# Expert stage of a hybrid layer: 128-column stationary tiles, a new order for the first two experts, filler products

## The chip, the core and the metric

The kernel runs on one core of one Trainium2 chip. The metric is the device time of one execution in microseconds. Its engines are named as in the profile: PE multiplies matrices, ACT and DVE work on tiles element by element, POOL and SP mostly issue transfers here, and 16 DMA engines move the data.

## What is computed

One transformer layer over 512 tokens of 1024 values in fp32: a gated linear attention, a sparse attention and an attention over a memory, mixed by gates, and then a mixture of 16 experts. The change lies in the mixture. Each token chooses one of four groups and two of its four experts, and the two experts' results are added with weights that come from the routing:

```
def _hier_moe(h, w_r1, b_r1, w_r2, b_r2, w_gate, w_up, w_down):
    ...
    g_sel = jnp.argmax(g_logits, axis=-1)
    ...
    top_p, top_i = lax.top_k(e_prob, EXPERT_TOPK)          # 2 of 4 in the group
    top_p = top_p / jnp.sum(top_p, axis=-1, keepdims=True)
    expert_id = g_sel[:, None] * EXPERTS_PER_GROUP + top_i
    combine = jnp.sum(jax.nn.one_hot(expert_id, N_EXPERTS, dtype=jnp.float32)
                      * (g_w * top_p)[..., None], axis=1)
    hid = jax.nn.silu(jnp.einsum('nd,edf->nef', hf, w_gate)) * jnp.einsum('nd,edf->nef', hf, w_up)
    hid = hid * combine[..., None].astype(hid.dtype)
    out = jnp.einsum('nef,efd->nd', hid, w_down)
```

The experts' hidden width is 256, so one expert has 1024 x 256 gate and up weights and 256 x 1024 down weights, 3 MB.

## The kernel before

**Split products.** Most products are made from fp32 values split into two parts of a shorter type, h and l (`split_into`, L92 to L99: ACT casts h, DVE subtracts to get l). `mm3` (L101 to L104) adds three PE products of such parts: h by h (L102), h by l (L103) and l by h (L104). In the trace's rows for the experts the stationary operand is named second: g<-wh,xgh is the PSUM tile g from the moving weights wh and the stationary tokens xgh, and "128*96" in such a row is 128 rows by 96 stationary columns. The gate stage of the attention part uses the same three products (L155, L160, L161) with 128 columns.

**Experts.** A routing stretch on PE, DVE and ACT (`route`, `place`, `weigh`, `spread`, `rows`, `weights`, L1107 to L1249) places each expert's tokens into C = 96 slots and writes their indices to `idx0` (L1243). For each expert `gather` (L1278) has POOL issue an indirect transfer that fetches the 96 token rows into one of two buffers. `tokens_t` (L1285) transposes them on PE in eight blocks (L1291) and splits the result, four blocks at a time, into xgh and xgl; the last block stays fp32 as xgr. `up` (L1311) runs one of four steps kc over the 1024 inputs: steps 0 to 2 are six split products each, step 3 is the fp32 products of xgr (L1323, two per expert, four records in the trace) and three split products. `hidden` (L1328) applies silu, the product and the routing weights `cwt0`, `hidden_t` (L1335) transposes the hidden values (L1338) and splits them into hh and hl, and `down` (L1344) makes six split products for each half c of the output. `scatter` (L1353) copies the result (ACT, L1355) and has POOL issue an indirect transfer that adds it into the output (L1356). So an expert has 21 + 12 = 33 split products. Expert 0's tokens come by products with one-hot matrices (L1172) and not by a gather, and its first PRE = 2 steps' weights are split ahead of time (eh, el).

**Order.** The scheduler of the language takes instructions in the order in which the loop over the experts emits them. A string of letters steers the loop (L1368 to L1393): a digit is a step of `up` for expert e, h its `hidden`, t `tokens_t` for expert e+1, and H, a, b are `hidden_t` and both halves of `down` for expert e-1; the last expert has a string of its own, LAST.

```
ORDER = "0H12at3bh"
...
            elif op == "t" and e + 1 < ne:
                xt[e + 1] = tokens_t(got[e + 1])
```

The routing weights (`weights`, L1245) come from four products (L1229) whose moving operand `aux` DVE makes (L1226), and are reduced by DVE to `cwt` (L1249). A count of tokens per expert (L1397) at the end decides whether a branch for more than 96 tokens runs; it does not run on these inputs. `WARM` = 8 products into an unused tile (`idle`, L1256) stand ahead of the last part of the routing.

**Weights.** `load_expert` (L858) issues an expert's 12 tiles of 256 KB on SP's queue, in order, into slots of one pool (tag "s", NS = 66, 2 KB a partition each); `fetch` runs NF = 4 experts ahead. The last HB = 2 tiles of expert 3 wait for `idx0` ("gathers first"), and all behind them in SP's queue with them. A tile is cast (L94) and split (L95) into one of WH = 3 pairs wh, wl. The tiles of tokens (tag "x", 4 buffers) and hidden values (tag "u", NU = 6) have as many columns as an expert has slots, 96.

## Time and profile before

| | us |
|---|---|
| median of 3 runs | 957.44 |
| lowest and highest run | 955.07, 958.75 |
| the profiled execution, its own time | 958.75 |
| its span in the trace | 957.0 |
| PE busy | 923.3 |
| DVE busy | 646.4 |
| ACT busy | 467.0 |
| POOL busy | 136.0 |

The profile is of one execution. A row of the timeline gives start and duration of an instruction in microseconds from the start of the span, its engine, its line in the kernel, what it writes from what it reads, its shape, and in brackets how long its engine stood idle ahead of it and what ended that. Matmuls are pipelined on PE, so the distance between the starts of two of them is the time that one takes, and the duration in the row is longer. A row of windows gives, for a stretch, the busy time and number of instructions of each engine, the granted clock of PE (1.00 is the full one), the share of the DMA engines' time that was in use, and what they moved.

### The profile page before, as it was taken

How to read it: one execution, taken by the hardware profiler on the slowest of the kernel's cores; microseconds unless marked ns; L12 is line 12 of the kernel's file. 1: busy time of each engine (PE TensorE's matmuls, PEld its weight loads, DVE VectorE, ACT ScalarE, POOL GpSimd, SP SyncE). 2: the span in 40 equal slices, each digit the busy share in tenths (PEclk: the TensorE clock that was granted, in tenths of full speed). 3: DMA queues.
4: the chain of work that ended last, by engine and by line, in shares of the span. 5: the costliest groups of instructions: out<-in, count | busy, mean ns of one | idle time of the engine just before them, and what ended most of it. 6: DMA issues, size and time to landing. Idle time of an engine off the chain costs nothing.

```text
span 957.0 us, 13025 instructions
## 1 busy us (share of the span) xinstructions
PE 923.3 (96%) x4408; PEld 747.7 (78%) x4408; DVE 646.4 (68%) x1602; ACT 467.0 (49%) x935; POOL 136.0 (14%) x120
## 2 busy tenths in 40 slices
PE   8898999999999999999999999999999988999994
PEld 5678888787888888887888888878888876777773
DVE  6785689869988595458545552573463667898983
ACT  5664546435323354455513423443324336888883
POOL 4000122000500050000000000000003122434332
PEclk9998999999999999999999999999999979999998
DMA  7744431312333223221332233215847439999992
GB/s 224 243 114 130 124 89 45 89 44 67 93 107 92 87 67 86 69 73 38 88 89 91 86 88 88 88 45 175 286 145 234 151 134 291 326 317 314 303 321 50
DMA packets 75063, 133.79 MB, mean 140 GB/s; under 512 B 10640, under 2 KB 13278, under 8 KB 74992
## 3 DMA queue, kind: packets, MB, share of 16 engines
q1 hardware_dynamic: 66656, 119.56, 39.9%
q0 software_dynamic: 7152, 11.25, 4.9%
q10 hardware_dynamic: 1184, 2.11, 0.6%
q8 instruction: 36, 0.59, 0.3%
q14 instruction: 35, 0.29, 0.1%
HBM read 125.59 MB, written 10.49 MB: 142 GB/s over the span
## 4 chain that ended last, share of the span: by engine, by line
PE 81%; DVE 9%; ACT 3%; DMA 3%; issue 2%; POOL 0%; SPq 0%; POOLq 0%; ACTq 0%; DVEq 0%
PE g L160 18%; PE g L155 18%; PE g L161 18%; PE g L104 4%; PE g L103 4%; PE g L102 4%; DVE wl L95 2%; PE g L1323 1%; PE tp L1291 1%; ACT wh L94 1%; PE g L1172 1%; DMA wr<-in_w_mem_kv_dram 1%; DMA hx<-in_x_dram 1%; PE tp L103 1%; PE lg L1095 1%
## 5 line engine op out<-in xcount | busy, mean ns | idle before, releaser
L94 ACT CAST wh<-wr 128x1024 fp32r<-128x1024 f32 (+2 forms) x125 | 127.6, 1024 | 277.5 <-PE g L160 160.6
L95 DVE TENSOR_TENSOR wl<-wr,wh 128x1024 fp32r<-128x1024 f32 (+2 forms) x125 | 152.3, 1220 | 154.1 <-ACT wh L94 152.6
L155 PE MATMUL g<-hh,wh 128*128 128x512 f32 (+1 forms) x424 | 167.7, 395 | 3.1 <-DVE mvl L98 1.9
L160 PE MATMUL g<-hl,wh 128*128 128x512 f32 (+1 forms) x424 | 166.1, 392 | 0.0
L161 PE MATMUL g<-hh,wl 128*128 128x512 f32 (+1 forms) x424 | 165.6, 391 | 0.0
L95 DVE TENSOR_TENSOR wl<-mw,wh 128x512 fp32r<-128x512 f32 (+1 forms) x188 | 112.6, 641 | 9.2 <-ACT wh L94 8.3
L94 ACT CAST wh<-mw 128x512 fp32r<-128x512 f32 (+1 forms) x188 | 100.9, 588 | 11.5 <-PE g L104 10.8
L155 PEld LDWEIGHTS g<-hh,wh 128*128 128x128 f32 x424 | 80.7, 190 | 18.4 <-DVE mvl L98 2.2
L161 PEld LDWEIGHTS g<-hh,wl 128*128 128x128 f32 x424 | 80.6, 190 | 15.1
L160 PEld LDWEIGHTS g<-hl,wh 128*128 128x128 f32 x424 | 80.7, 190 | 14.1
L160 PE MATMUL g<-wl,hh 128*128 128x512 f32 x160 | 63.1, 394 | 0.0
L155 PE MATMUL g<-wh,hh 128*128 128x512 f32 x160 | 63.1, 394 | 0.0
L161 PE MATMUL g<-wh,hl 128*128 128x512 f32 x160 | 62.9, 393 | 0.0
L1356 POOL DMA_INDIRECT out_dram<-y,idx x32 | 45.5, 1421 | 91.3 <-ACT y L1355 87.4
L102 PE MATMUL g<-wh,xgh 128*96 128x512 f32 x108 | 46.7, 433 | 0.0
L476 POOL PARTITION_ALL_REDUCE dqsq<-dqsq x8 | 26.3, 3364 | 127.0 <-ACT dqsq L468 127.0
L104 PE MATMUL g<-wh,xgl 128*96 128x512 f32 x108 | 42.8, 397 | 0.0
L103 PE MATMUL g<-wl,xgh 128*96 128x512 f32 x108 | 42.6, 395 | 0.0
L987 POOL MEMSET tmp<- 128x128 f32 x1 | 0.2, 206 | 290.8 <-PE tp L822 290.8
L160 PEld LDWEIGHTS g<-wl,hh 128*128 128x128 f32 x160 | 30.2, 189 | 6.2 <-issue 0.5
L155 PEld LDWEIGHTS g<-wh,hh 128*128 128x128 f32 x160 | 30.1, 188 | 6.3 <-issue 0.5
L645 ACT ACTIVATE dp<-dp,nm,rs_y 128x128 f32<-128x128 f32 (+3 forms) x32 | 20.9, 654 | 28.5 <-DVE nm L644 28.5
(424 smaller groups left out, 1991.9 us busy)
## 6 DMA issues: line engine op xcount, KB each, us to landing
wr<-in_w_in_dram SPq DMA_DIRECT2D x72, 512.0 KB, 3.5
mw<-in_w_gate_dram SPq DMA_DIRECT2D x64, 256.0 KB, 7.6
mw<-in_w_up_dram SPq DMA_DIRECT2D x64, 256.0 KB, 7.8
mw<-in_w_down_dram SPq DMA_DIRECT2D x64, 256.0 KB, 7.5
wr<-in_w_mem_kv_dram SPq DMA_DIRECT2D x16, 512.0 KB, 6.3
wr<-in_w_o_mem_dram SPq DMA_DIRECT2D x8, 512.0 KB, 3.6
wr<-in_w_o_dsa_dram SPq DMA_DIRECT2D x8, 512.0 KB, 3.6
wr<-in_w_o_gla_dram SPq DMA_DIRECT2D x8, 512.0 KB, 4.2
```

The costliest lines, as they stand in the source:

```text
L94: hi = A.copy(h, src)
L95: lo = V.tensor_sub(l, src, h.bitcast(F32))
L102: PE.matmul(ps, sh, mh, start=first, stop=False)
L103: PE.matmul(ps, sh, ml, start=False, stop=False)
L104: PE.matmul(ps, sl, mh, start=False, stop=last)
L155: i = PE.matmul(ps, sh, mh, start=first, stop=False)
L160: PE.matmul(ps, sh, ml, start=False, stop=False)
L161: i = PE.matmul(ps, sl, mh, start=False, stop=last)
L476: G.partition_all_reduce(flat, flat, P, bass_isa.ReduceOp.add)
L645: A.activation(p, p, AF.Exp, bias=nm[:, t:t + 1], scale=rs, accum_out=sm[:, t:t + 1])
L1095: PE.matmul(pl, hT[:, k, :], wr[:, kb, :], start=k == 0, stop=k == 3)
L1356: nc.gpsimd.indirect_dma_start(out=out[c], in_=y, in_offset=None, compute_op=OP.add, out_offset=bass.IndirectOffsetOnAxis(ap=idx0[:, e:e + ...
```

## The change

The stationary tiles of tokens and hidden values become buffers that are allocated once, with 128 columns, of which the last 32 are set to zero once (seven memsets on DVE); every product of `up` and `down` now has 128 stationary columns, and its PSUM tile 128 rows, of which the first 96 are read. `tokens_t` becomes a generator of two parts: t makes the eight transposes and splits the first four blocks, u splits the rest. There are strings of their own for expert 0 (FIRST) and expert 1 (SECOND), so that all of expert 0's steps come ahead of expert 1's transposes. Those transposes, and WARM = 4 filler products ahead of them, are held behind the last product of expert 0's step 3 and the last product of the routing weights (`after_all`). The 8 idle products ahead of the routing remain. The weights' pool grows from 66 to 72 slots; for that the space for the descriptors of indirect transfers is cut from 16384 bytes a partition, the default, to 4096.

```diff
@@ -31,14 +31,14 @@
 TAKEN = -(2.0 ** 127)
 NEG = -1e30
 
-NS, NU, WR, WH = 66, 6, 4, 3
+NS, NU, WR, WH = 72, 6, 4, 3
 AHEAD, NF = 2, 4
 E0, HB = -1, 2
-ORDER = "0H12at3bh"
+FIRST, SECOND, ORDER = "0123htu", "Ha012bt3uh", "0H12at3ubh"
 LAST = "0H12a3hbGcd"
 N1, N2 = 8, 8
 PRE = 2
-WARM = 8
+WARM = 4
 L0, L2, LW, LA = 2, 2, 2, 2
 SB, MS, MB, D1, D2, DB, GS = 12, 3, 6, 12, 10, 16, 9
 WA, WB = 12, 17
@@ -101,7 +101,7 @@
     def mm3(ps, sh, sl, mh, ml, first, last):
         PE.matmul(ps, sh, mh, start=first, stop=False)
         PE.matmul(ps, sh, ml, start=False, stop=False)
-        PE.matmul(ps, sl, mh, start=False, stop=last)
+        return PE.matmul(ps, sl, mh, start=False, stop=last)
 
     def wconv(raw, w):
         h = wp.tile([P, 2, w], F32R, tag="wh", name="wh", bufs=WH)
@@ -1226,8 +1226,9 @@
         V.tensor_mul(aux, sel[:, tt, :, :].rearrange("p t c e -> p (t c) e").to_broadcast([P, 4, 16, n]),
                      vals[:, tt, :, o:o + n].rearrange("p t c v -> p (t c) v")[:, :, None, :].to_broadcast([P, 4, 16, n]))
         for k in range(4):
-            PE.matmul(ps, ohs[t0 // 2][:, k, :], aux[:, k, :, :].rearrange("p e c -> p (e c)"),
+            end = PE.matmul(ps, ohs[t0 // 2][:, k, :], aux[:, k, :, :].rearrange("p e c -> p (e c)"),
                       start=t0 == 0 and k == 0, stop=last and t0 == 2 and k == 3)
+        return end
 
     def rows(idx):
         pi = ap_.tile([C, 16 * 3], F32, tag="lg", name="lg")
@@ -1245,14 +1246,15 @@
     def weights(ohs, cwt):
         pw = ap_.tile([C, 16 * 6], F32, tag="lg", name="lg")
         for t0 in (0, 2):
-            spread(pw, ohs, 3, 6, t0, True)
+            end = spread(pw, ohs, 3, 6, t0, True)
         V.tensor_reduce(cwt, pw.rearrange("p (e q c) -> p e q c", q=2, c=3), axis=AX.X, op=OP.add)
+        return end
 
     out_gemm()
     run(fill[0])
 
     idle = gp.tile([P, 512], F32, tag="g", name="g")
-    for _ in range(WARM):
+    for _ in range(8):
         PE.matmul(idle, mgH[0][:, 0:P], mgH[0], start=True, stop=True)
     rest = place(2)
     run(islice(rest, N2))
@@ -1282,31 +1284,38 @@
                                      bounds_check=T - 1, oob_is_err=False)
         return xb[e % 2]
 
+
+    xs = [[sp.tile([P, 4, P], F32R, tag="x", name="xg" + n, bufs=4) for n in "hl"] for _ in range(2)]
+    xraw = sp.tile([P, P], F32, tag="xr", name="xgr", bufs=1)
+    hhl = [half([P, 2, P], F32R, "h" + n) for n in "hl"]
+    for t in xs[0] + xs[1] + hhl:
+        V.memset(t[:, :, C:P].bitcast(F32), 0.0)
+    V.memset(xraw[:, C:P], 0.0)
+
     def tokens_t(xg, placed=None, m=C):
+
         xH, xL = [], []
+        tps = placed
+        if placed is None:
+            tps = [ap_.tile([P, 4, m], F32, tag="tp", name="tp") for _ in range(2)]
+            for kb in range(KB):
+                PE.transpose(tps[kb // 4][:, kb % 4, :], xg[:, :, kb], ident[0:m, 0:m])
         for c in range(2):
-            if placed is None:
-                tp = ap_.tile([P, 4, m], F32, tag="tp", name="tp")
-                for k in range(4):
-                    PE.transpose(tp[:, k, :], xg[:, :, 4 * c + k], ident[0:m, 0:m])
-            else:
-                tp = placed[c]
-            h = sp.tile([P, 4, m], F32R, tag="x", name="xgh", bufs=4)
-            l = sp.tile([P, 4, m], F32R, tag="x", name="xgl", bufs=4)
-            raw = sp.tile([P, m], F32, tag="xr", name="xgr", bufs=2) if c else None
+            tp = tps[c]
+            h, l = xs[c]
             n = 4 - c
             if placed is None:
-                split_into(h[:, 0:n, :], l[:, 0:n, :], tp[:, 0:n, :])
+                split_into(h[:, 0:n, 0:m], l[:, 0:n, 0:m], tp[:, 0:n, :])
             else:
                 for k in (0, 2):
                     q = min(k + 2, n)
-                    split_into(h[:, k:q, :], l[:, k:q, :], tp[:, k:q, :])
-            if c:
-                A.copy(raw, tp[:, n, :])
+                    split_into(h[:, k:q, 0:m], l[:, k:q, 0:m], tp[:, k:q, :])
             xH += [h[:, k, :] for k in range(4)]
             xL += [l[:, k, :] for k in range(4)]
-        xL[KB - 1] = raw
-        return xH, xL
+            if c:
+                A.copy(xraw[:, 0:m], tp[:, n, :])
+                xL[KB - 1] = xraw
+            yield xH, xL
 
     def up(ps, xH, xL, ws, kc, done=None):
         nk = 1 if kc == 3 else 2
@@ -1323,28 +1332,28 @@
                 PE.matmul(ps[:, i * 256:(i + 1) * 256], xL[KB - 1], ws[4 * i + kc][:, 1, :], start=False, stop=False)
         for k in range(nk):
             kb = 2 * kc + k
-            mm3(ps, xH[kb], xL[kb], *parts[k], kb == 0, kc == 3)
+            end = mm3(ps, xH[kb], xL[kb], *parts[k], kb == 0, kc == 3)
+        return end
 
     def hidden(ps, cwt, m=C):
         hid = half([m, P, 2], F32, "hid")
         hf = hid.rearrange("p i k -> p (i k)")
-        A.activation(hf, ps[:, 0:256], AF.Silu, scale=cwt[:, 1:2])
-        V.scalar_tensor_tensor(hf, ps[:, 256:512], cwt[:, 0:1], hf, op0=OP.mult, op1=OP.mult)
+        A.activation(hf, ps[0:m, 0:256], AF.Silu, scale=cwt[:, 1:2])
+        V.scalar_tensor_tensor(hf, ps[0:m, 256:512], cwt[:, 0:1], hf, op0=OP.mult, op1=OP.mult)
         return hid
 
     def hidden_t(hid, m=C):
         tp = ap_.tile([P, 2, m], F32, tag="tp", name="tp")
         for k in range(2):
             PE.transpose(tp[:, k, :], hid[:, :, k], ident[0:m, 0:m])
-        hh = half([P, 2, m], F32R, "hh")
-        hl = half([P, 2, m], F32R, "hl")
-        split_into(hh, hl, tp)
+        hh, hl = hhl
+        split_into(hh[:, :, 0:m], hl[:, :, 0:m], tp)
         return hh, hl
 
-    def down(hh, hl, ws, c, m=C):
+    def down(hh, hl, ws, c):
         wh = wp.tile([P, 2, 512], F32R, tag="wh", name="wh", bufs=WH)
         wl = wp.tile([P, 2, 512], F32R, tag="wl", name="wl", bufs=WH)
-        ps = gp.tile([m, 512], F32, tag="g", name="g")
+        ps = gp.tile([P, 512], F32, tag="g", name="g")
         for k in range(2):
             split_into(wh[:, k, :], wl[:, k, :], ws[8 + 2 * c + k])
             mm3(ps, hh[:, k, :], hl[:, k, :], wh[:, k, :], wl[:, k, :], k == 0, k == 1)
@@ -1352,7 +1361,7 @@
 
     def scatter(e, c, ps):
         y = yb[e % 2][:, c, :]
-        A.copy(y, ps)
+        A.copy(y, ps[0:C, :])
         nc.gpsimd.indirect_dma_start(out=out[c], in_=y, in_offset=None, compute_op=OP.add,
                                      out_offset=bass.IndirectOffsetOnAxis(ap=idx0[:, e:e + 1], axis=0),
                                      bounds_check=T - 1, oob_is_err=False)
@@ -1363,27 +1372,35 @@
     with tc.issue_after(late[LW].ins):
         weigh(2)
     with tc.issue_after(late[LA].ins):
-        weights(ohs0, cwt0)
-    xt[0] = tokens_t(None, x0)
+        weighed = weights(ohs0, cwt0)
+    xt[0] = list(tokens_t(None, x0))[1]
     for e in range(ne):
         if e + NF < ne:
             fetch(e + NF, after=found if e == E0 else None)
         if e + 2 < ne:
             got[e + 2] = gather(e + 2)
-        for op in ORDER if e < ne - 1 else LAST:
+        for op in {0: FIRST, 1: SECOND, ne - 1: LAST}.get(e, ORDER):
             if op in "0123":
                 if op == "0":
-                    ps = gp.tile([C, 512], F32, tag="g", name="g")
+                    ps = gp.tile([P, 512], F32, tag="g", name="g")
                 kc = int(op)
                 if e == 0 and kc >= PRE:
                     with tc.issue_after(late[2].ins):
-                        up(ps, *xt[e], wts[e], kc)
+                        end = up(ps, *xt[e], wts[e], kc)
                 else:
                     up(ps, *xt[e], wts[e], kc, pre if e == 0 else None)
             elif op == "h":
                 hid[e] = hidden(ps, cwt0[:, e, :])
             elif op == "t" and e + 1 < ne:
-                xt[e + 1] = tokens_t(got[e + 1])
+                with after_all([end, weighed] if e == 0 else []):
+                    if e == 0:
+                        for _ in range(WARM):
+                            PE.matmul(idle, xs[0][0][:, 0, :], xs[0][0].rearrange("p k c -> p (k c)"),
+                                      start=True, stop=True)
+                    halves = tokens_t(got[e + 1])
+                    xt[e + 1] = next(halves)
+            elif op == "u" and e + 1 < ne:
+                next(halves)
             elif op in "HabGcd" and e + (op in "Gcd") > 0:
                 o = e if op in "Gcd" else e - 1
                 if op in "HG":
@@ -1422,7 +1439,7 @@
                 V.tensor_copy(cx, cw[:, t, one, :].rearrange("p o q -> p (o q)"))
                 xg = wp.tile([P, P, KB], F32, tag="wr", name="xg", bufs=WR)
                 nc.sync.dma_start(xg.rearrange("p i k -> p (i k)"), h2d[rs, :])
-                xH, xL = tokens_t(xg, m=P)
+                xH, xL = list(tokens_t(xg, m=P))[1]
                 ps = gp.tile([P, 512], F32, tag="g", name="g")
                 for kc in range(4):
                     up(ps, xH, xL, ws, kc)
@@ -1430,7 +1447,7 @@
                 for c in range(2):
                     o = slot([P, 512], F32, "o")
                     nc.sync.dma_start(o, out[c][rs, :])
-                    V.tensor_add(o, o, down(hh, hl, ws, c, P))
+                    V.tensor_add(o, o, down(hh, hl, ws, c))
                     nc.sync.dma_start(out[c][rs, :], o)
 
 
@@ -1445,7 +1462,8 @@
     import concourse.bacc as bacc
     from concourse.bass_utils import run_bass_kernel_spmd
 
-    nc = bacc.Bacc("TRN2", target_bir_lowering=False, num_devices=1)
+    nc = bacc.Bacc("TRN2", target_bir_lowering=False, num_devices=1,
+                   dynamic_dma_scratch_size=4096)
     arrays, args = {}, {}
     for name in _INS:
         v = np.ascontiguousarray(np.asarray(inputs[name])[0])
```

Three places show how the instructions move. On PE, behind step kc 2 of expert 0, before the change (lg<-aux are the products of the routing weights, tp<-ident,xg the transposes of expert 1's tokens, and the numbers are the stationary columns by the moving ones; transposes are listed the other way round):

```order
L104 MATMUL g<-wh,xgl 96x512
L1291 MATMUL tp<-ident,xg 128x96 x8
L1323 MATMUL g<-mw,xgr 96x256 x2
L102 MATMUL g<-wh,xgh 96x512
L103 MATMUL g<-wl,xgh 96x512
L104 MATMUL g<-wh,xgl 96x512
L102 MATMUL g<-wh,xgh 96x512
L1229 LDWEIGHTS oh
L1229 MATMUL lg<-aux_7255,oh 96x96
```

On PE at the same place after the change (L1414 is the count, L1398 the fillers, L1302 the transposes of expert 1's tokens and L1348 those of expert 0's hidden values):

```order
L1414 LDWEIGHTS ones_b
L1414 MATMUL lg<-sel_6454,ones_b 128x16
...
L1332 MATMUL g<-mw,xgr 128x256 x2
L102 MATMUL g<-wh,xgh 128x512
L103 MATMUL g<-wl,xgh 128x512
L104 MATMUL g<-wh,xgl 128x512
L1229 LDWEIGHTS oh
L1229 MATMUL lg<-aux_7269,oh 96x96
...
L1398 MATMUL g<-xgh 128x512 x4
L1302 MATMUL tp<-ident,xg 128x96 x8
L1348 MATMUL tp<-ident,hid 128x96 x2
L102 MATMUL g<-wh,hh 128x512
```

The count comes from the end of the kernel to this place, the transposes of expert 1 go behind expert 0's step kc 3, the products of the routing weights and the fillers, and the down products of expert 0 come right behind, ahead of all of expert 1's steps.

On DVE in the same stretch, before the change (aux_7255 is the operand of the routing weights' last products, pr and vals are parts of the routing):

```order
L1208 TENSOR_TENSOR pr<-pr,vals 128x4
L95 TENSOR_TENSOR wl<-mw,wh 128x2x256
L1209 CAST vals<-pr 128x4
L95 TENSOR_TENSOR xgl<-tp,xgh 128x384
L1226 TENSOR_TENSOR aux_7255<-sel,vals 128x384
L95 TENSOR_TENSOR wl<-mw,wh 128x2x256
L1249 TENSOR_REDUCE cwt_7136<-lg 96x32
L95 TENSOR_TENSOR xgl<-tp,xgh 128x288
```

On DVE after it (cmaxi is the highest count, hl the lower part of the hidden values):

```order
L1208 TENSOR_TENSOR pr<-pr,vals 128x4
L95 TENSOR_TENSOR wl<-mw,wh 128x2x256
L1209 CAST vals<-pr 128x4
L1418 CAST cmaxi<-cmax 128x1
L1226 TENSOR_TENSOR aux_7269<-sel,vals 128x384
L95 TENSOR_TENSOR wl<-mw,wh 128x2x256
L1250 TENSOR_REDUCE cwt_7136<-lg 96x32
L95 TENSOR_TENSOR wl<-mw,wh 128x2x256
L1342 SCALAR_TENSOR_TENSOR hid<-g,cwt_7136,hid 96x256
L95 TENSOR_TENSOR xgl<-tp,xgh 128x4x96
L95 TENSOR_TENSOR xgl<-tp,xgh 128x3x96
L95 TENSOR_TENSOR hl<-tp,hh 128x2x96
```

The operand of the routing weights no longer stands behind the split of expert 1's tokens, and both halves of that split stand directly ahead of the split of expert 0's hidden values.

## Rows read from the trace of the kernel before

**Rows 1.** The page, busy time of each engine, its share and number of instructions:

```profile
PE 923.3 (96%) x4408; PEld 747.7 (78%) x4408; DVE 646.4 (68%) x1602; ACT 467.0 (49%) x935; POOL 136.0 (14%) x120
```

**Rows 2.** Windows of the expert stage: PE, PEld, DVE, ACT, POOL, clock, DMA, GB/s:

```profile
820.00:840.00 20.00, 20.00 (x99) 14.79 (x98) 18.00 (x34) 17.53 (x40) 7.89 (x6) 1.00 1.01 323
936.00:938.00 2.00, 2.00 (x10) 1.43 (x9) 1.75 (x4) 1.51 (x3) 0.00 (x0) 1.00 0.26 56
```

**Rows 3.** Timeline of PE: transposes of experts 2 and 15, first product of expert 2:

```profile
803.32 1.02 PE L1291 MATMUL tp<-ident,xg 96*128 96x96 f32 x8
804.18 1.03 PE L1323 MATMUL g<-mw,xgr 128*96 128x256 f32 x4
804.86 0.58 PE L102 MATMUL g<-wh,xgh 128*96 128x512 f32 x1
...
807.13 0.39 PE L102 MATMUL g<-wh,xgh 128*96 128x512 f32 x1
...
927.86 1.02 PE L1291 MATMUL tp<-ident,xg 96*128 96x96 f32 x8
```

**Rows 4.** Timeline of PE, head of the expert stage:

```profile
787.22 0.40 PE L102 MATMUL g<-eh,xgh 128*96 128x512 f32 x1
...
790.46 0.39 PE L104 MATMUL g<-wh,xgl 128*96 128x512 f32 x1
793.25 1.30 PE L1291 MATMUL tp<-ident,xg 96*128 96x96 f32 x8 [2.40 <-DMA xg<-h2d,idx]
...
797.34 0.39 PE L102 MATMUL g<-wh,xgh 128*96 128x512 f32 x1
```

**Rows 5.** Windows of the head, columns as in rows 2:

```profile
790.00:794.00 4.00, 1.59 (x10) 1.07 (x9) 1.79 (x7) 0.62 (x1) 0.00 (x0) 0.99 0.89 220
794.00:796.00 2.00, 2.00 (x9) 1.47 (x7) 1.46 (x3) 1.00 (x2) 0.96 (x1) 0.50 0.98 296
```

**Rows 6.** Timeline of PE, gate stage, first and last of 37 products in a row:

```profile
742.59 0.39 PE L155 MATMUL g<-wh,mgh 128*128 128x512 f32 x1
...
750.78 0.39 PE L155 MATMUL g<-wh,mgh 128*128 128x512 f32 x1
```

**Rows 7.** Groups of loads, 720 to 957: count, busy us, mean ns, idle before:

```profile
L103 PEld LDWEIGHTS g<-wl,xgh 128*96 128x96 f32 x108 | 17.6, 163 | 6.4
...
L155 PEld LDWEIGHTS g<-wh,mgh 128*128 128x128 f32 x54 | 10.2, 188 | 1.7
```

**Rows 8.** Timeline of DVE in the head:

```profile
794.54 0.56 DVE L95 TENSOR_TENSOR xgl<-tp,xgh 128x384 fp32r<-128x384 f32 x1 [2.22 <-ACT xgh L94]
795.01 0.55 DVE L1226 TENSOR_TENSOR aux<-sel,vals 128x384 bf16<-128x384 bf16 x1
```

**Rows 9.** Timeline of POOL, issue of the gather for expert 1:

```profile
786.24 1.33 POOL L1280 DMA_INDIRECT xg<-h2d,idx  x1 [15.91 <-DVE rr L1208]
```

**Rows 10.** Waits of SP's queue, 785 to 800: total us, times, longest:

```profile
SPq L866 <- PE tp L1291: 2.4, 1, 2.4
```

**Rows 11.** Timeline of SP, issue of a weight tile of expert 15:

```profile
923.02 0.33 SPq L866 DMA_DIRECT2D mw<-in_w_up_dram  x1
```

**Rows 12.** The page, transfers: count, KB each, median us from issue to landing:

```profile
mw<-in_w_up_dram SPq DMA_DIRECT2D x64, 256.0 KB, 7.8
```

**Rows 13.** Timelines of ACT and PE, expert 15's step kc 1:

```profile
931.54 0.63 ACT L94 CAST wh<-mw 128x512 fp32r<-128x512 f32 x1
...
933.21 0.45 PE L102 MATMUL g<-wh,xgh 128*96 128x512 f32 x1
```

**Rows 14.** Timeline of DVE in the routing stretch:

```profile
781.47 0.22 DVE L1153 TENSOR_TENSOR ppc<-sel,lg 128x64 f32<-128x64 bf16 x1 [2.65 <-PE lg L1151]
```

**Rows 15.** Timeline of PE, last head of the sparse attention:

```profile
429.78 0.55 PE L662 MATMUL tp<-ident,dp 128*128 128x128 f32 x3 [0.25 <-DVE dol L95]
```

**Rows 16.** Waits, 800 to 940, columns as in rows 10:

```profile
DVE wl L95 <- DMA mw<-in_w_gate_dram: 0.6, 2, 0.3
```

**Rows 17.** Scatters by their line, L1356: time to landing in the whole span:

```profile
DMA to landing us min/median/max: 4.1/7.0/8.0
```

## Prediction

> **What bounds the kernel now.** I read the page first: PE is busy for 923.3 of 957.0 us [rows 1], so time can only come from PE's own work or from the few places where it stands still. The change touches two stretches. In the expert stage PE is full, 20.00 us of 20, while the DMA engines are full as well, share 1.01 at 323 GB/s [rows 2]. One expert takes (927.86 - 803.32) / 13 = 9.58 us on PE, from one expert's transposes to the next one's [rows 3]. The other stretch is the head of that stage: the last split product of expert 0's step kc 2 starts at 790.46, and the next thing in PE's row, expert 1's transposes, at 793.25, after 2.40 us of idle time put down to the gather of expert 1's tokens [rows 4]. [...]
>
> What that head costs: from 793.25 to 797.34 PE ran eight transposes, the fp32 products and three split products in 4.09 us [rows 4]. At the full clock the transposes and fp32 products of expert 2 took 804.86 - 803.32 = 1.54 us [rows 3], and three split products take 0.69, so 2.23 us. The slow clock costs 1.86 us and the idle time 2.40, together 4.3 us. No more than that can be had in the head.
>
> **The change part by part.**
>
> *128 columns.* Products with 96 stationary columns follow each other by (790.46 - 787.22) / 14 = 231.4 ns [rows 4]; products of the gate stage with 128 columns by (750.78 - 742.59) / 36 = 227.5 ns [rows 6]. There are 33 split products per expert, 528 in all; 528 x 3.9 ns = 2.1 us less. Zero is the other end, if the 4 ns belong to the gate stage and not to the columns; I take 2.0, since operation, type and moving size are the same. The load of the stationary tile gets longer, from 163 to 188 ns in the mean [rows 7]. If the 25 ns came on top, they would cost 528 x 25 = 13 us; but both loads are shorter than the spacing, and with 188-ns loads the gate stage still kept 227.5 ns, so they lie beside the products. [...]
>
> *Head.* Expert 0's last products, the count of tokens per expert and the products that gather the routing weights go ahead of expert 1's transposes, and four filler products stand behind them. I walk PE's row from 790.69, where 790.46's slot ends. Four count products cost at most 0.43 us, since expert 2's eight transposes start 0.86 us ahead of its fp32 products [rows 3]. Then kc 3 of expert 0: 1.54 - 0.86 = 0.68 for the fp32 products and 0.69 for three split ones, to 792.5. The weight products need an operand from DVE. Before, that ran at 795.01, behind a split that had waited 2.22 us for the transposed tokens and began at 794.54 [rows 8]; so DVE was free at 792.3. In the new order one more split and three short operations are ahead of it, and it is ready at 793.1 to 793.7: PE waits some 0.9 us. Four weight products take at most 0.43 again, four fillers 0.91, and the transposes begin at 794.7, when the gather has landed, if it is issued at 786.24 [rows 9] and lands by 793.25 as before; they end at 795.6. ACT and DVE then split two halves of the tokens and the hidden values in turn, so the first down product waits about 0.7 us, to 796.3 (an estimate from the 0.56 us of one half's split [rows 8]). Thirty products at 0.2275 are 6.8 us, transposes and fp32 products 1.54, three products 0.69: expert 2's first product comes at 805.4 instead of 807.13 [rows 3]. That is 1.7 us, of which 0.14 (36 products by 3.9 ns) is in the 2.0 above already. The stretch also had small waits that the walk leaves out, so I take 1.3 us. The high end is 1.6; the low end is -0.3, if the two waits bring the half clock back as the 2.40 us did (1.86 us). What is late next is the split of the hidden values.
>
> *72 slots for weights.* In the head SP waited once, for 2.4 us, for PE's transposes to free a slot [rows 10], and the DMA share was 0.89 in 790 to 794 [rows 5]. Six more slots of 256 KB let SP issue past that. To be had is the missing share, 0.11 of 4 us, 0.4 us, since from 794 on it is 0.98 and over. I take 0.4 (the other end is 0): earlier weights, not yet an earlier end.
>
> *The cap.* PE's gain is 2.0 + 1.3 = 3.3 us. But the weights come at the rate of the DMA engines, which are full nearly to 936 (1.01 in 820 to 840, 0.26 in 936 to 938 [rows 2]); a PE that is 3.3 us ahead would meet them. At expert 15 the kc 1 tile of in_w_up was issued at 923.02 [rows 11], and with the median of 7.8 us to landing [rows 12] it came at about 930.8. ACT cast it at 931.54, and PE started on that step at 933.21 [rows 13]. A cast at the landing would let PE come 0.7 us earlier, and some 0.4 of the 1.67 between cast and step can go (the cast is 0.63, and DVE's half of the split about as long): 1.1 us in all, and 0.4 from the slots. So 1.5 of the 3.3 us reach the end; the ends are 0 and 3.7 (2.1 + 1.6).
>
> *Costed at nothing.* Seven memsets of padding columns run on DVE, most of them in the routing stretch, where it stood idle for 2.65 us ahead of 781.47 [rows 14]; if all fell on the way to the gather's indices they would cost 7 x 0.19 = 1.3 us (an estimate: a third of the 384-column split's 0.56). The second half of the token split moves behind kc 3, which reads the same buffers, so it could not run sooner. In the last head of the sparse attention, near 430 us, the scheduler spreads filler work differently; PE waits there for 0.25 us at a time [rows 15], and two such waits, 0.5 us either way, are my allowance. The count leaves the tail, where PE waited for the hidden values anyway.
>
> **The sum.** The profiled run took 958.75 us (span 957.0). Less 1.5 it is 957.2. The median of the runs, 957.44, stands 1.3 below the profiled run; less 1.5 it is 955.9 us.
>
> **Rivals.**
>
> *The weights do not bind.* Their last tiles come sooner than the median or the casts close up, and all 3.3 us stay: 954.1. For it: in 800 to 940 DVE waited for gate tiles only twice, 0.6 us in all [rows 16]. Against it: the full DMA share.
>
> *It doesn't do what it says.* The idle time goes over from the gather to the weight operand and the hidden split, at the half clock, and the 4 ns are not the columns': 957.4 + 0.3 = 957.7, and up to 959.5 with memsets (1.3) and the reorder (0.5). For it: the walk has PE waiting 1.6 us in place of 2.40. Against it: the spacings in rows 4 and 6 differ steadily over 14 and 36 products.
>
> *Everything lands.* The whole 4.3 us of the head less 0.9 for the fillers, 2.1 from the columns and no cap: 5.5 us, 951.9. It needs the weight operand and the hidden split on time; the walk has them 0.9 and 0.7 late.
>
> *Slower: GpSimd's transfers queue for descriptor space.* The change cuts the space for descriptors of indirect transfers from 16384 to 4096 bytes a partition. The place is POOL's queue, with two scatters and a gather per expert. If one must land before the next is written, each costs its way to landing, 7.0 us in the median for a scatter [rows 17]; three are 21 us, 11.4 over the 9.58 of an expert, and 14 experts add 160 us: some 1115. With two in flight three take 10.5 us, 0.9 over, and add 13 us: 970. It decides from 3.2 us per transfer. Against it: POOL is busy for 7.89 of 20 us [rows 2], so it has room, but nothing shows how full the space is. [...]
>
> **How the numbers follow.** Chances: the capped forecast 0.50, no cap 0.20, no effect 0.14, everything lands 0.10, slower through the descriptors or a load that is not hidden 0.06. A measurement of this kernel can tell about 0.5%, 4.8 us, from no change: under 952.65 counts as faster, over 962.2 as slower. Faster is most of the case where everything lands and the low edge of the uncapped one, 0.12; slower is 0.07 with the edge of no effect; the same 0.81. The range goes from 951.5 (everything lands, with 0.4 from the reorder near 430 us) to 959.5 (no effect, with memsets and reorder); it leaves out the descriptor case and edges of the others.
>
> **What the profile of the changed kernel would show.** PE's idle time ahead of expert 1's transposes should be near 1 us and owed to DVE, no window after 790 should show 0.50, and expert 2's first product should start between 805.3 and 806. Products should follow each other by 227 to 228 ns, an expert take 9.45 us, and then, in the last three experts, ACT or DVE should wait for gate and up weights: that is the cap. If there are no such waits and PE ends 3 us earlier, the cap is wrong. If 0.50 stays in 794 to 800, the head is wrong; if the spacing stays at 231, the columns give nothing; if POOL waits for DMA between gathers, the descriptors are short, and the forecast is wrong by most.

## The result and the profile after

The changed kernel took 948.63 us in the median of 7 runs (947.74 to 953.18), the kernel before 957.44 (955.07 to 961.52) in 7 runs beside them: ratio 0.9905, 95% interval 0.9887 to 0.9923, so 8.8 us faster. The forecast was 955.9, "the same", with a range down to 951.5. The time lies below the range.

The profiled run of the changed kernel was the longest of its seven (953.18 us, span 951.24). Its first products of the memory attention began at 10.86 us where they began at 8.51 before, and from there on it ran late. So the same kernel was run once more ("after_r" below: 949.5 us in the median, and 949.5 in its profiled run, span 947.57), and the rows "of after" come from that profile, unless the text says otherwise.

The page of after, busy times and granted clock in 40 slices:

```profile
PE 917.9 (97%) x4412; PEld 756.3 (80%) x4412; DVE 645.4 (68%) x1609; ACT 467.8 (49%) x935; POOL 136.5 (14%) x120
...
PEclk9999999999999999999999999999999999999998
```

The same line of the page of before, which the prediction did not use:

```profile
PEclk9998999999999999999999999999999979999998
```

PE's busy time fell by 5.4 us against [rows 1]; its weight loads grew by 8.6 us and lie beside the products. The 7 in slice 33 (some 765 to 789 us: the routing of the last token tiles, ahead of the expert stage) is gone. The prediction began its account of PE at 786 and passed over this slice. (The 8 in slice 4 comes and goes from run to run: the first profile of the changed kernel has it too.)

Both profiles, cut at the same instructions on PE (us; each cell is a difference of two starts in the timeline):

| stretch | before | after | difference |
|---|---|---|---|
| start to the last gate product ahead of the last routing products | 765.37 | 763.75 | -1.6 |
| routing: from there to expert 0's first product | 21.10 | 15.20 | -5.9 |
| head: from there to expert 3's transposes | 26.43 | 26.13 | -0.3 |
| expert 3's transposes to the last product | 131.15 | 133.76 | +2.6 |
| last product to the last scatter's issue | 3.89 | 2.52 | -1.4 |
| last scatter's issue to the end of the span | 9.02 | 6.21 | -2.8 |

The first line says nothing of the change: the changed kernel's own two profiles stand at 768.25 and 763.75 there. The gain lies in the routing and behind the last scatter, two places for which the prediction had no gain at all.

*The routing.* Windows of before, columns as in [rows 2] (PE, PEld, DVE, ACT, POOL busy, clock, DMA share, GB/s), and the same windows of after:

```profile
764.00:768.00 4.00, 1.90 (x11) 1.28 (x10) 3.79 (x16) 1.23 (x6) 3.21 (x5) 1.00 0.71 229
768.00:772.00 4.00, 3.65 (x26) 3.44 (x27) 2.95 (x26) 3.83 (x13) 1.84 (x2) 0.75 0.82 295
772.00:776.00 4.00, 4.00 (x21) 4.00 (x20) 0.99 (x10) 0.00 (x0) 0.00 (x0) 0.50 0.46 180
```

```profile
764.00:768.00 4.00, 3.33 (x30) 2.97 (x30) 3.21 (x23) 4.00 (x14) 1.84 (x2) 1.00 0.45 177
768.00:772.00 4.00, 4.00 (x33) 3.82 (x33) 2.72 (x27) 0.31 (x1) 0.00 (x0) 1.00 0.09 35
772.00:776.00 4.00, 2.66 (x24) 2.14 (x23) 3.47 (x22) 0.00 (x0) 0.00 (x0) 1.00 0.00 0
```

Before, PE stood still for more than half of 764 to 768, and then worked at a granted clock of 0.75 and 0.50. After, it did neither. The timelines of before tell why it stood still: POOL, DVE, ACT and PE, one fence each.

```profile
761.76 2.53 POOL L1077 TENSOR_TENSOR xg<-xr,gffn 128x512 f32<-128x512 f32 x2 [19.12 <-PE g L160]
...
765.37 1.28 POOL L1077 TENSOR_TENSOR xg<-xr,gffn 128x512 f32<-128x512 f32 x1
```

```profile
762.01 1.05 DVE L1182 TENSOR_SCALAR neg<-gt 128x2 f32<-128x2 f32 x1
...
763.17 1.14 DVE L1122 TENSOR_TENSOR sg<-slots,gf 128x8 f32<-128x8 f32 x1
...
765.30 1.38 DVE L1183 TENSOR_SCALAR neg<-et 128x2 f32<-128x2 f32 x1
```

```profile
766.77 0.30 ACT L1190 ACTIVATE gexp<-es,neg 128x4 f32<-128x4 f32 x1 [2.77 <-DVE ef L1133]
...
767.26 0.56 ACT L1085 COPY h2T<-tp 128x512 f32<-128x512 f32 x1
```

```profile
767.88 1.07 PE L1095 MATMUL lg<-wr__6407,h2T 128*128 128x24 f32 x8 [2.10 <-ACT h2T L1085]
```

The tile `xg` of `residual` (L1075), the scaled token rows on their way to `h2d`, is taken from the same pool of slots as the expert weights. POOL waited 19.12 us for a slot, until a gate product released a weight. So its products fell on DVE's top-2 chain of the routing: three steps of a few elements took 1.05 to 1.38 us, each until the POOL product beside it had ended (halfway through the pair, 763.03; 764.29; 766.65). ACT ran the copy of the transposed tokens (767.26) behind L1190 (766.77, after a wait of 2.77 us for DVE), and PE waited 2.10 us for that copy.

After, POOL has its slots early, and its products run one by one as DVE gives their inputs (of four, the last three stand here); before, the first three of the same four fell into 761.76 to 766.65. Then DVE and PE:

```profile
754.02 1.29 POOL L1077 TENSOR_TENSOR xg<-xr,gffn 128x512 f32<-128x512 f32 x1 [2.33 <-DVE xr L1074]
...
759.68 1.28 POOL L1077 TENSOR_TENSOR xg<-xr,gffn 128x512 f32<-128x512 f32 x1 [3.49 <-DVE xr L1074]
...
764.97 1.26 POOL L1077 TENSOR_TENSOR xg<-xr,gffn 128x512 f32<-128x512 f32 x1 [3.13 <-DVE xr L1074]
```

```profile
759.75 1.25 DVE L1112 SCALAR_TENSOR_TENSOR lt<-lp,rt_y,br 128x24 f32<-128x24 f32 x1
...
763.01 0.15 DVE L1183 TENSOR_SCALAR neg<-et 128x2 f32<-128x2 f32 x1
```

```profile
764.35 1.07 PE L1095 MATMUL lg<-wr__6407,h2T 128*128 128x24 f32 x8 [0.20 <-ACT h2T L1085]
```

L1183 takes 0.15 us, and PE's wait is 0.20. Two meetings are left, and they cost little: L1112 with POOL's product of 759.68, ahead of that wait of 0.20, and the first step of L1167 with that of 764.97 (0.39 us, 0.26 before), behind which PE waits 0.47 us where it waited 0.35. Of the 5.9 us, 1.9 are the wait (2.10 to 0.20); the other 4.0 lie where the clock was 0.75 and 0.50 and is now 1.00.

The three steps end within 0.03 us of the POOL products: at 763.06, 764.31 and 766.68, where these end at 763.03, 764.29 and 766.65. In the first profile of the changed kernel, with no POOL product beside them, the same three take 0.15, 0.17 and 0.15 us. And L1112, 0.24 us before with no product beside it, takes 1.25 us after and ends 0.04 us behind the one of 759.68. That the product holds the step up is read from these times; by what means, no trace shows.

*The end.* The closing drain on POOL's queue, of before and of after (count, shortest, median and longest in ns, first and last start in us):

```profile
L1456 POOLq DRAIN  x3: 52/115/7625, 948.5 to 956.7; - x3
```

```profile
L1474 POOLq DRAIN  x3: 52/115/4721, 942.0 to 947.3; - x3
```

It is 2.9 us shorter, and the span ends with it. (The 1.4 us ahead of it are the last scatter's wait for the landing of the scatter before it: 2.34 us before, 0.99 after, 1.68 in a_warm0 and 1.89 in a_order0. Why it lands sooner stays open.)

### The profile page after: what moved, and what is told of

Its sections match the earlier page's. It is cut to its first block, busy times and chain, and to the rows that moved or that the text cites. A ratio compares the mean times of both kernels' runs of the same rounds, so it can differ in the third digit from the quotient of the medians.

```text
span 951.2 us, 13022 instructions
## 1 busy us (share of the span) xinstructions
PE 920.1 (97%) x4412; PEld 759.2 (80%) x4412; DVE 645.4 (68%) x1609; ACT 467.7 (49%) x935; POOL 136.6 (14%) x120
## 4 chain that ended last, share of the span: by engine, by line
PE 80%; DVE 9%; ACT 4%; DMA 3%; issue 2%; POOL 0%; SPq 0%; POOLq 0%; ACTq 0%; DVEq 0%
PE g L160 19%; PE g L155 19%; PE g L161 19%; PE g L102 4%; PE g L104 4%; PE g L103 4%; DVE wl L95 2%; ACT wh L94 1%; PE tp L1302 1%; PE g L1332 1%; DMA mw<-in_w_gate_dram 1%; DMA wr<-in_w_mem_kv_dram 1%; PE tp L662 1%; PE tp L103 1%; DMA hx<-in_x_dram 1%
## 5 line engine op out<-in xcount | busy, mean ns | idle before, releaser
L161 PEld LDWEIGHTS g<-hh,wl 128*128 128x128 f32 x424 | 80.6, 190 | 15.2
L102 PE MATMUL g<-wh,xgh 128*128 128x512 f32 x108 | 46.5, 431 | 0.7 <-ACT wh L94 0.7
L103 PE MATMUL g<-wl,xgh 128*128 128x512 f32 x108 | 42.5, 393 | 0.3 <-DVE wl L95 0.3
L104 PE MATMUL g<-wh,xgl 128*128 128x512 f32 x108 | 42.5, 393 | 0.0
L161 PEld LDWEIGHTS g<-wh,hl 128*128 128x128 f32 x160 | 30.1, 188 | 6.2 <-issue 0.2
```

Source lines behind the costliest of these rows:

```text
L102: PE.matmul(ps, sh, mh, start=first, stop=False)
L103: PE.matmul(ps, sh, ml, start=False, stop=False)
L104: return PE.matmul(ps, sl, mh, start=False, stop=last)
L161: i = PE.matmul(ps, sl, mh, start=False, stop=last)
```

## The experiments

All runs, with the ratio to the kernel before on the same chip; n is the number of timed runs, "routing", "head" and "rest" the second to fourth lines of the table above, and "drain" the longest drain of POOL's queue, all in us from the run's one profile. The profiled run is not always the median, so a stretch is compared where it decides, and the time by the ratio.

| run | what | median (n) | ratio [95%] | routing | head | rest | drain |
|---|---|---|---|---|---|---|---|
| b_scratch | before, 4096 bytes | 955.43 (12) | 0.997 [0.9957, 0.9984] | 21.1 | 28.5 | 131.2 | 4.8 |
| b_slots | before, 4096, 72 slots | 951.09 (6) | 0.992 [0.9898, 0.9942] | 19.3 | 27.0 | 131.2 | 4.8 |
| b_xgown | before, 4096, own buffers for xg | 949.7 (6) | 0.9913 [0.9883, 0.9942] | 14.7 | 27.9 | 131.2 | 4.9 |
| b_fill | before, 4096, 8 fillers in the routing | 955.67 (12) | 0.9981 [0.9966, 0.9996] | 20.1 | 26.5 | 131.2 | 4.9 |
| a_ns66 | changed, 66 slots | 954.06 (6) | 0.9948 [0.9929, 0.9968] | 20.9 | 26.1 | 131.3 | 4.7 |
| a_s16 | changed, 66 slots, 16384 | 957.28 (12) | 0.9986 [0.9972, 1.0] | 22.2 | 27.7 | 131.9 | 7.4 |
| a_order0 | changed, old order of the first experts, no fillers | 949.55 (6) | 0.9908 [0.9888, 0.9927] | 15.2 | 25.2 | 133.6 | 5.0 |
| a_warm0 | changed, no fillers | 950.59 (6) | 0.9931 [0.9908, 0.9954] | 15.2 | 27.1 | 131.8 | 4.8 |
| a_less | changed, 4 tiles not loaded | 947.47 (6) | 0.9882 [0.9863, 0.9901] | 15.2 | 26.1 | 130.8 | 4.8 |
| a_free | changed, no loads held for idx | 948.89 (6) | 0.991 [0.9889, 0.9931] | 15.2 | 26.5 | 130.9 | 4.9 |
| a_free0 | a_free, old order, no fillers | 950.11 (12) | 0.9937 [0.9915, 0.996] | 15.2 | 26.9 | 130.8 | 4.8 |
| after_r | changed, again | 949.5 (5) | 0.9915 [0.989, 0.9941] | 15.2 | 26.1 | 133.8 | 4.7 |
| b_s8 | before, 8192 | 955.02 (1) | | 20.9 | 25.7 | 131.8 | 4.6 |
| b_s12 | before, 12288 | 956.21 (1) | | 20.6 | 28.3 | 131.2 | 7.0 |

**Parts alone: the space and the slots.** b_scratch and b_slots add them to the kernel before, a_ns66 takes the slots out of the changed one.

```
b_scratch:  + dynamic_dma_scratch_size=4096
b_slots:    + dynamic_dma_scratch_size=4096
            - NS, NU, WR, WH = 66, 6, 4, 3
            + NS, NU, WR, WH = 72, 6, 4, 3
a_ns66:     - NS, NU, WR, WH = 72, 6, 4, 3
            + NS, NU, WR, WH = 66, 6, 4, 3
```

> The kernel before, with the descriptor space of the indirect transfers cut from 16384 to 4096 bytes and nothing else; its instructions stand in the same order on every engine. The profiles of before and after differ behind the last scatter: POOL's closing drain took 7.6 us before (948.5 to 956.1) and 4.8 us after (945.6 to 950.4). Theory 'descriptor space': the drain gets shorter with the space alone, by some 2.9 us, so 954.5 us here. Rival 'tail by chance': the drain ends with the last transfers and differs from run to run, so 957.4 us here and a drain of 7 us or more. Rival 'short space' of the prediction: POOL's transfers wait for each other, slower than 957.4.

> The kernel before with 72 slots and the small descriptor space, no other edit. Theory 'slots serve the routing': the tiles that POOL writes between the normalisation and the routing (L1077) come from the same pool as the weights; POOL waited 19.1 us for one before and 8.1 us after. With 72 slots POOL runs earlier, no longer into DVE's routing steps, PE's wait of 2.10 us ahead of the routing products at 767.9 shrinks to under 0.5 us and the half clock of 770 to 780 is gone: 5 to 6 us less than the run with the small space alone, some 949 us. Rival 'late start': the profiled run of after had begun 3 us late on PE, and the wait closed for that reason alone; then this kernel takes as long as the one with the small space alone, with the clock at 0.50 in 770 to 780.

> The changed kernel with 66 slots in place of 72; columns, order, fillers and the small descriptor space stay. Theory 'slots serve the routing': the wait and the half clock of the routing stretch come back, 5 to 6 us more than the changed kernel, some 954 us. Rival 'late start': no difference from the changed kernel's 948.6 us beyond what the slots give in the head (0.4 us).

The space alone gave 3 us, the slots 4.3 more, and the changed kernel without its slots lost 3 to 4 of its 8.8 us (0.9948 against 0.9915 in after_r and 0.9905). Its routing stretch has the old wait and the old clock back (PE's timeline, then windows of a_ns66):

```profile
768.79 1.07 PE L1095 MATMUL lg<-wr__6407,h2T 128*128 128x24 f32 x8 [2.12 <-ACT h2T L1085]
```

```profile
772.00:776.00 4.00, 4.00 (x21) 4.00 (x20) 0.52 (x6) 0.76 (x2) 0.00 (x0) 0.50 0.72 279
```

b_slots has the wait gone (0.21 us), but its profiled run fell to the half clock all the same:

```profile
772.00:776.00 4.00, 4.00 (x21) 4.00 (x20) 3.02 (x26) 0.00 (x0) 0.00 (x0) 0.50 0.01 2
```

Its six runs part by the mean granted clock: 953.54 and 955.3 us at 0.986 to 0.987, 952.49 and 948.41 at 0.990, 949.02 and 949.69 at 0.994 to 0.995. So the wait and the clock are two things, and between the lowest and the highest of these clocks lie some 5 us.

**More weights ahead, or free slots for xg?** b_xgown gives xg eight buffers of its own and leaves the weights two slots fewer than before.

```
- NS, NU, WR, WH = 66, 6, 4, 3
+ NS, NU, WR, WH = 64, 6, 4, 3
-        xg = slot([P, 512], F32, "xg")
+        xg = sp.tile([P, 512], F32, tag="xq", name="xg", bufs=8)
+ dynamic_dma_scratch_size=4096
```

> The kernel before with the small descriptor space, 64 slots for weights and the rest, and a pool of its own of 8 buffers for the tiles that POOL writes ahead of the routing (L1077): as much memory as 72 slots, but weights have no more than before. Theory 'slots serve the routing': POOL no longer waits for a weight's slot, so as fast as 72 common slots: 951 us or less, PE's wait ahead of the routing products under 0.5 us. Rival 'more weights ahead': the slots helped by the weights that they hold, so no better than the small space alone, 955.4 us.

Routing fell to 14.7 us. POOL's timeline in b_xgown has the product at its early place, waiting for DVE's input only:

```profile
760.48 1.29 POOL L1077 TENSOR_TENSOR xg<-xr,gffn 128x512 f32<-128x512 f32 x1 [3.44 <-DVE xr L1074]
```

Weights further ahead are excluded: there were fewer slots for them. With these edits alone the kernel before comes to 0.9913, where the whole change came to 0.9905.

**Is it the clock, and do fillers keep it up?** b_fill puts eight idle products where PE waited 2.10 us.

```
+        if (t, c) == (NT - 2, 1):
+            warm = gp.tile([P, 512], F32, tag="g", name="warm")
+            for _ in range(8):
+                PE.matmul(warm, mgH[0][:, 0:P], mgH[0], start=True, stop=True)
+ dynamic_dma_scratch_size=4096
```

> The kernel before with the small descriptor space and, new, eight idle products of 512 columns ahead of the routing products that PE waited 2.10 us for (at 767.0 in the run with the small space alone); 66 slots. They cost 8 x 0.228 = 1.8 us inside that wait, so nothing by themselves. Theory 'the wait costs by the clock behind it': the windows from 768 to 780 run at 1.00 in place of 0.50; the eight routing and idle products there no longer take twice as long, and the run takes some 3.5 us less than the 955.4 of the small space alone, 952. Rival 'POOL's earlier start is what counts, not the clock': the wait stays as the end of the same chain, 955.4.

Nothing was gained over b_scratch, and the run is inconclusive on the clock. The fillers filled the wait (0.28 us left), but the edit also changed the order on DVE, and PE waited later on; PE's timeline in b_fill:

```profile
772.71 2.51 PE L1176 MATMUL g<-oh,xg 128*128 128x96 f32 x11 [2.63 <-DVE oh L1171]
```

What it does show: with the first wait filled by idle products, and a clock of 1.00 up to 772, the routing was 20.1 us and the run no faster, since another wait for DVE came behind it.

**The head: the new order and the fillers.** a_order0 takes both out, a_warm0 the fillers alone.

```
a_order0:  - FIRST, SECOND, ORDER = "0123htu", "Ha012bt3uh", "0H12at3ubh"
           + FIRST, SECOND, ORDER = "012t3uh", "0H12at3ubh", "0H12at3ubh"
           - WARM = 4
           + WARM = 0
           - with after_all([end, weighed] if e == 0 else []):
           + with after_all([]):
a_warm0:   - WARM = 4
           + WARM = 0
```

> The changed kernel without the new order of the first two experts and without fillers (strings 012t3uh and 0H12at3ubh, nothing held); slots, descriptor space, 128 columns and the two halves of the token split stay. Theory of the prediction for the head: the order is worth 1.3 us, so 950.0 us, with 2.4 us of PE waiting for the gather and 0.50 behind it. Theory from the two traces: in the changed kernel the head gained only 0.3 us against before (its start is 3.0 us earlier, expert 2's first product 3.3 us), so 949.0 us. Rival 'order is the change': back at 955 or more.

> The changed kernel without the four filler products (0.9 us of PE ahead of expert 1's transposes); the order stays. Theory 'the fillers hold the clock': without them PE stands longer ahead of the transposes, the clock falls to 0.50 behind them, and expert 2's start comes 1 us later: 949 to 950 us. Rival 'the wait for weights near the end takes it all': 948.6 whatever the head does, and the head without fillers is shorter by up to 0.9 us where the clock stays at 1.00.

a_order0 kept the whole gain: 949.55, between the 950.0 and the 949.0 of the two theories, which it cannot part. In its profile the transposes wait for the gather again, as in [rows 4], yet with a full clock:

```profile
786.32 1.13 PE L1302 MATMUL tp<-ident,xg 96*128 96x96 f32 x8 [2.73 <-DMA xg<-h2d,idx]
```

a_warm0 ran at 0.78 to 0.79 in 788 to 796, and its median was 1.1 us over after_r's, with intervals that overlap:

```profile
788.00:792.00 4.00, 2.34 (x12) 1.82 (x12) 2.56 (x7) 1.59 (x5) 0.96 (x1) 0.79 1.01 290
792.00:796.00 4.00, 4.00 (x15) 3.18 (x14) 0.67 (x2) 1.80 (x4) 0.94 (x1) 0.78 1.03 331
```

The "head" column puts them in order. In the old order eight of nine profiles (that of before among them) had a clock of 0.50 to 0.57 in at least one of the three windows of 2 us from the start of expert 1's transposes, and the head took 25.7 to 28.5 us (26.4 in the one that the prediction read); the ninth, a_order0, stayed at 1.00 and took 25.2. The new order with its fillers stayed at 1.00 in five of six profiles (both of the changed kernel among them), 26.1 to 26.5 us, and fell to 0.50 in one (a_s16, 27.7); without fillers it fell and took 27.1. So the new order at the full clock was slower than the old one in its only profile at the full clock, by 0.9 us: its own waits and fillers cost as much as the wait for the gather. What it buys is that the clock mostly stays up. The means are 26.9 and 26.5 us, 0.4 to 0.5 apart.

**The cap by the weights.** a_less leaves part of the work out: the four down tiles of expert 12 are not loaded, and expert 11's are used in their place. a_free lets no tile of the later experts wait for the routing's indices. a_free0 is a_free with the old order and without fillers.

```
a_less:   + if kept and i >= 8:
          +     ws[i] = kept[i]
a_free:   - E0, HB = -1, 2
          + E0, HB = -1, 0
a_free0:  the edits of a_free and of a_order0
```

> The changed kernel, in which expert 12's four down tiles are not loaded; expert 11's are used in their place, so 1 MB less of 50 is moved in the expert stage, and expert 12 gives another result. No work of PE, DVE or ACT changes. Theory 'cap': in the changed kernel ACT waited 2.3 us for a gate tile near 918, and the last experts took 11.56 us instead of 9.55; 1 MB is 3.2 us of the DMA engines' time, so that wait goes and the run ends some 2 us earlier, 946.6. Rival 'no cap' (the wait is one late transfer, by chance): 948.6, no change.

> The changed kernel in which no weight tile waits for the gathers' indices (HB = 0): SP waited 19.6 us for them, and the DMA engines stood at shares of 0.00 to 0.18 from 772 to 784. Theory 'cap': expert 4's tiles and the slots' worth behind them come in that hole, the waits on weights near 918 go, and the run ends 2 us earlier, 946.6. Rival 'gathers first': the weights are in the gather's way, expert 1's tokens land later than at 791.8, PE waits for them in the head, and the gain is given back: 948.6 or more.

> The changed kernel with no weight tile waiting for the gathers' indices, and without the new order and the fillers. Theory 'cap': in the run with the order kept and no tile waiting, PE had no wait on weights any more; with the old order the head was 0.9 us shorter where the clock stayed up, so 947 us, 1.5 us under the changed kernel. Rival 'gathers first': the gather lands later behind the weights, PE waits for it over 2.7 us with the half clock behind it: 950 us.

Waits of after, 800 to 940 us (who waits and for what; total, times, longest), then the timelines of ACT, at the cast that waits, and of PE, the transposes of experts 14 and 15:

```profile
ACT wh L94 <- DMA mw<-in_w_gate_dram: 2.4, 1, 2.4
...
PE g L102 <- ACT wh L94: 0.8, 1, 0.8
```

```profile
913.69 1.14 ACT L94 CAST wh<-mw 128x512 fp32r<-128x512 f32 x2 [2.42 <-DMA mw<-in_w_gate_dram]
```

```profile
910.12 1.02 PE L1302 MATMUL tp<-ident,xg 96*128 96x96 f32 x8
...
921.80 1.02 PE L1302 MATMUL tp<-ident,xg 96*128 96x96 f32 x8
```

Expert 14 took 11.68 us where the experts ahead of it took 9.55. In a_less and a_free ACT waits for no gate tile in that stretch, expert 14 takes 9.55 us, and "rest" is 130.8 to 130.9 us instead of 133.8. So the late tiles cost 2.9 us in this trace (2.0 in the first profile of the changed kernel). (The 3.2 us for 1 MB in what was expected of a_less are an estimate: 1 MB at the 317 GB/s that before moved in a window of 100 us, shown further below.) In time a_less came to 0.9882, below after_r's 0.9915 and after's 0.9905, though the intervals overlap; a_free, which loads everything, came to 0.991: PE's gain there is lost again within the spread, and its head was 0.4 us longer. a_free0 missed its 947 us: 950.11, as its rival had it. PE waits 2.74 us for the gather there, with a clock of 0.50 behind it; the wait is as long as the 2.73 us of a_order0, so the loads were not in the gather's way. So the wait for weights is shown, and that its removal helps the whole is not.

**The same kernel again.**

> The changed kernel once more, unchanged, as the reference on the same chip for the three others: 948.6 us, clock 0.99 or more.

The first line of the stretches came out at 763.75 instead of 768.25, the rest alike: the late start belonged to that run.

**The closing drain against the space.** b_s8 and b_s12 are the kernel before with other sizes, a_s16 is a_ns66 without the reduced space.

```
b_s8:   + dynamic_dma_scratch_size=8192
b_s12:  + dynamic_dma_scratch_size=12288
a_s16:  - NS, NU, WR, WH = 72, 6, 4, 3
        + NS, NU, WR, WH = 66, 6, 4, 3
        - dynamic_dma_scratch_size=4096
```

> The kernel before with a descriptor space of 8192 bytes, between 16384 (POOL's closing drain 7.6 us) and 4096 (4.8 us in four kernels). Theory 'the drain goes with the size of the space': 7.6 - 2.8 x 8/12 = 5.7 us. Rival 'a threshold' (some state that only the full space reaches): 4.8 or 7.6 us.

> The kernel before with a descriptor space of 12288 bytes; 16384 gave a closing drain of 7.6 us, 8192 one of 4.6, 4096 one of 4.8. Theory 'a threshold': either 4.6 to 4.9 us or 7 us and more. Rival 'it goes with the size': between them, some 6 us.

> The changed kernel with 66 slots and the full descriptor space of 16384 bytes: columns, order and fillers alone. Theory 'descriptor space': POOL's closing drain is back at 7 us or more, and the run takes 2.5 to 3 us longer than the changed kernel with 66 slots and the small space (954.1), 957 us, no better than before. Rival 'the order of the last scatters shortens the drain': 4.8 us and 954 us.

The drain in b_s8, b_s12 and a_s16, one fence each:

```profile
L1457 POOLq DRAIN  x3: 52/115/4611, 947.9 to 953.0; - x3
```

```profile
L1457 POOLq DRAIN  x3: 52/115/7001, 946.7 to 954.2; - x3
```

```profile
L1473 POOLq DRAIN  x3: 52/115/7373, 949.1 to 957.0; - x3
```

It does not grow in proportion: 4.7 to 5.0 us at 4096, 4.6 at 8192, 7.0 at 12288, 7.4 and 7.6 at 16384. Why there is a step between 8192 and 12288 stays open. a_s16 against a_ns66, 0.9986 to 0.9948, gives the space 3.6 us in the changed kernel, as b_scratch gave it 3 in the old one.

No run beat the changed kernel by more than the intervals; a_less, which leaves work out, came nearest to it.

## Why the prediction was wrong

The direction of its mechanisms was right where it looked; the time came from two terms that it had as 0.4 and as nothing. Its first sentence already hid both: it looks for time in PE's work and PE's waits, but busy time does not tell the half clock from the full one (in 772 to 776 of before PE was busy for 4.00 of 4 us at 0.50, in 768 to 772 of after for 4.00 of 4 us at 1.00), and the drain stands behind PE's last product.

1. *The slots: the step that failed.* They were costed by the DMA share in the head, 0.4 us. The runs give them some 4 (b_slots against b_scratch, the changed kernel against a_ns66), in the routing stretch. The prediction asked what more slots let SP issue, not who else draws from the pool. The rows for it were there: POOL's 19.12 us ahead of its product is put down to a release by PE, the window 772 to 776 shows 0.50, and the page's clock line a 7. It even used a DVE row of that stretch [rows 14], as room for memsets.
2. *The descriptor space.* It stood in the rivals as a way to be slower. POOL's queue did not choke (in every run at 4096 a scatter was issued 0.28 us behind the end of the copy that it sends, in the median, as before, and apart from the last at most 0.74 us), and the drain gave 3 us. The tail behind the last scatter was not read. It could not have been priced from the trace of before, but 7.6 us of drain stood in it.
3. *The columns: right in sign, mis-sized.* 2.0 us were forecast. PE's timeline of after, the transposes of two experts eight apart:

```profile
805.08 0.47 PE L1302 MATMUL tp<-ident,xg 96*128 96x96 f32 x3
...
881.46 1.02 PE L1302 MATMUL tp<-ident,xg 96*128 96x96 f32 x8
```

   That is 9.55 us per expert, 9.58 before: 0.03 each, 0.4 in all. In the traces the start of an L104 product does follow that of its L103 product after 227 ns instead of 230 to 231, the 4 ns of the forecast; but the step from an L102 product of `up` to its L103 product (267 ns in the mean before, 271 after) and the one between fp32 products (217 before, 226 after) got longer. The step that failed carried the spacing of 14 products in a row [rows 4] over to all 33. That the longer loads are hidden was right. Loads of after by line, as in [rows 7]:

```profile
L103 PEld LDWEIGHTS g<-wl,xgh 128*128 128x128 f32 x108 | 20.4, 189 | 5.4 <-DVE wl L95 1.8
```

4. *The head: the waits that were looked for were there, and one was missed.* The weight operand was forecast 0.9 us late and was 1.03. PE's timeline of after:

```profile
786.10 0.34 PE L1229 MATMUL lg<-aux,oh 128*96 128x96 bf16 x4 [1.03 <-DVE aux L1226]
786.26 1.18 PE L1398 MATMUL g<-xgh 128*128 128x512 f32 x4
787.28 1.02 PE L1302 MATMUL tp<-ident,xg 96*128 96x96 f32 x8
...
789.08 0.48 PE L1348 MATMUL tp<-ident,hid 96*128 96x96 f32 x2 [0.77 <-DVE xgl L95]
...
789.96 0.50 PE L102 MATMUL g<-wh,hh 128*128 128x512 f32 x1 [0.41 <-ACT hh L94]
```

   The gather's wait is gone and the clock stayed at 1.00, as forecast, where [rows 5] has 0.50 in 794 to 796 (the slow clock of the prediction's 1.86 us). From the end of expert 0's kc 2 (783.15) to the transposes it is 4.13 us, where the walk had 4.0. The step that failed is the next one. The walk let the first down product wait 0.7 us behind the transposes. But the hidden values have two transposes of their own (L1348), which wait 0.77 us until the first half of the token split has ended (789.02): they need a PSUM tile `tp`, the kernel has two (bufs=2), and the token transposes fill both. The down product then waits 0.41 more for their split: 1.82 us from the end of the token transposes (787.28 + 0.86) to 789.96. With two smaller misses behind it, of 0.15 and 0.2, expert 2's first product (799.34) comes 16.19 us after kc 2, where the walk had 14.7 and before 16.44. So 0.3 us instead of 1.3.
5. *The cap: the wait came, but not by the lead that the sum gave it.* An expert's first gate tile was late, and 2.6 us went back. But the 5.9 us of the routing are no lead over the loads. SP's first load behind the routing's indices went out 0.46 us ahead of expert 0's first product before (786.47) and 0.45 us ahead of it after (778.95); SP's timelines, before and after:

```profile
786.01 0.80 SPq L871 DMA_DIRECT2D mw<-in_w_down_dram  x2
```

```profile
778.50 1.03 SPq L871 DMA_DIRECT2D mw<-in_w_down_dram  x2
```

   Counted from that product, PE reached expert 14's transposes 131.2 us behind it, 0.65 earlier than before (131.8), while expert 14's first gate tile landed 134.7 us behind it, 5.4 later than before (129.3). The DMA engines were as full as before and moved less; windows of 100 us, before and after, each from 13 us behind that product:

```profile
799.50:899.50 100.00, 100.00 (x493) 74.25 (x492) 89.59 (x169) 87.72 (x198) 39.42 (x30) 1.00 1.02 317
```

```profile
792.00:892.00 100.00, 100.00 (x496) 84.79 (x495) 89.24 (x166) 88.11 (x198) 39.39 (x30) 1.00 1.01 308
```

   b_xgown, whose loads go out as early (778.89), moved 315 GB/s in that stretch and has no such wait. So the step that failed is the one that took the landing times of the loads from the trace of before, and PE's gain as all that changes. Why the loads were slower after stays open, and what the cap would take from a lead of 3.3 us no run shows.
6. *Costed at nothing.* The memsets and the order near 430 us left nothing that the runs show. The rest of the change without slots and space is a_s16: 0.9986, 1.3 us and at most 2.7; "the same", as forecast for it. That this comes near the forecast's 1.5 us is luck: in its profile the routing, the head and the rest were longer than before, by 1.1, 1.3 and 0.7 us, and the wait between the last product and the last scatter's issue was 1.5 us shorter.

The chances put 0.81 on no change. They were fair for the parts that were costed; no rival was "another user of the pool", and the range ended at 951.5 since everything that could land was counted in the head and the columns alone.

## What to carry to other kernels

When a pool gets more buffers, list every tile that draws from it, and look for each one's longest wait for a slot, on all engines; a 19-us wait of an engine that is 14% busy can set when its work falls on somebody else's chain. Before a gain of one engine is set against its loads, see what releases the loads: here the same indices released both. Read the clock line of the page slice by slice, and cost each low slice before the stretch that the change is named after. And time a setting alone that looks like a risk only: the descriptor space was worth a third of the gain.
